# Neighbourhood-attention rows prepared for the output projection inside the retention stage, their value shares added by a small accumulating transfer per unit

## The chip, the cores and the metric

One core of one Trainium2 chip runs one whole layer of a hybrid diffusion backbone. The metric is the device time of that one launch in microseconds, taken as the median of several runs. The kernel before stands at 1739.89 us (three runs, 1737.87 to 1741.62).

## The reference, cut to what matters

The layer takes 1024 latent tokens of width 1024 and 256 context tokens. One input projection feeds two branches and two sets of gates; the branches are merged, projected and followed by a gated feed-forward network with a short convolution.

```
hx  = modulate(rmsnorm(x, norm1_g), sh1, sc1)             # 1024 x 1024
q, k, v, rq, rk, rv, rg, ga, gb = split(hx @ w_in)
o_na  = neighbourhood_attention(q, k, v, context k and v)  # 8 heads of 64: 1024 x 512, rows divided by the softmax sum
o_ret = norm(bi_retention(rope(rq), rope(rk), rv)) * silu(rg)   # 4 heads, chunks of 128
merged = sigmoid(ga) * (o_na @ w_proj_na) + sigmoid(gb) * (o_ret @ w_proj_ret)
x = x + g1 * (merged @ w_out)
x = x + g2 * conv_ffn(modulate(rmsnorm(x, norm2_g), sh2, sc2))
return rmsnorm(x, final_norm_g)
```

The change concerns `o_na`: how it gets from the attention to the product `o_na @ w_proj_na`.

## The kernel before, in words

Everything is kept transposed: channels on the 128 partitions, tokens along the free axis. A product in full fp32 precision is made of three TensorE (PE) matmuls: each operand is split into a rounded part ("hi", a copy to the type fp32r) and the rest ("lo", the difference), and hi·hi, hi·lo and lo·hi are summed. `split` (L90) does it, with the cast on ScalarE (ACT, L91) and the subtraction on VectorE (DVE, L92). `wload` (L102) fetches a 128x512 piece of a weight into a `raw` tile (three buffers, an SP transfer, L96) and splits it into a `wc` tile; `mm_a` (L121) runs such a product with the weights stationary (L115 to L117), `mm3` (L126 to L128) is a single product.

Stages in order of time: norms and adaLN (to 103 us), attention (103 to 370), retention (370 to about 690, with the gate columns of the input projection mixed into its last part), `pn` = `o_na @ w_proj_na` (702 to 754), the silu and merge gates (from 754), merge and output projection, feed-forward.

**Attention.** Four pairs of heads (`NPAIR`) by eight blocks of 128 tokens (`NJ`) give 32 units. A unit's values matmul yields, for two heads, a tile `rs` of 128 partitions: rows 0 to 63 and rows 64 to 127 are two shares of the same 64 channels (one from the hi, one from the lo half of V), which are to be added, and which lie in different partitions. `output` (L524 to L527) sends the two halves by two SP transfers of 64 KB to two planes of `d_ona` in DRAM. `rs` has two buffers. The softmax sums' reciprocals go to `d_r`.

**Retention.** Four heads of ten chunks: a `slot` (L1280) takes one front chunk of a head (projections, rotation, transposes, state products) together with one mixing chunk of the head before it; about 8 us each. In the front, ACT and DVE scale the keys into a tile `kz` (L1166 to L1171, two buffers) for the state product `dS` (L1173). The generator `shares` (L1264 to L1278) is advanced by one step per slot. Its first four steps each issue an accumulating POOL transfer of 512 KB that adds plane 1 of `d_ona` to plane 0 in DRAM. Its next sixteen steps handle eight pieces of 128x512: one step loads the sum (`osum`) and the reciprocals, spread over 64 partitions each (`rrep`), the next multiplies them on DVE (L1276) and writes the product back (L1277, a transfer on ACT's queue).

**Start of pn.** After the retention, eight loads `onr` (L1384) bring the scaled rows to SBUF in the column order of the gate stage (each row in pieces of 64 floats), and then all eight pieces are split in a row, ACT casting (L1388) and DVE subtracting (L1389), both with a permuting read (`perm`). The two `ona` tiles hold 128 x 4 x 1024 each. The loop (L1514 to L1533) then makes, for each of eight output blocks `db` and two halves of the tokens, twelve matmuls into a PSUM tile `pn`; the tile is multiplied by a gate `sgt` (loaded from `d_gate`, sigmoid on ACT) or copied, and stored in `d_pn`. Inside the loop `hx_sums` (L1365) makes the sums of blocks of hx for the Strassen-like gate products that follow: 4 POOL additions, 4 DVE additions and 4 splits, four times; its operands `hxT` are first read by PE right after pn's end.

**Order.** A list scheduler places the instructions of each engine ahead of time from modelled costs; those wrapped in `late` stay in the order in which they are written. Each engine then runs its own list strictly in order and waits for semaphores. DMA issues are instructions in such a list too: SP carries nearly all loads and stores, ACT some stores, POOL the accumulating ones. Pools are stacks of SBUF space: a pool opened later may take the space of a released one and then waits for its last users. `hcpool` holds the normalised context, which the retention still reads.

The rows that read kz and ona on PE:

```
for d in need:
    act.activation(kz[:, d, 0], k, AF.Copy, scale=self.dec(d))
    ...
    mm3(dS[:, d], kz[:, d, 0], kz[:, d, 1], v[:, 0], v[:, 1], True, True)
```

Of the kernel before, what the change touches and what calls it, by code (L numbers as in the profile page):

```python
# [8 lines left out]
F32 = mybir.dt.float32  # L9
F32R = mybir.dt.float32r  # L10
AF = mybir.ActivationFunctionType
ALU = mybir.AluOpType
# [4 lines left out]
P = 128  # L17
D = 1024
KB = D // P
T = 1024  # L20
# [5 lines left out]
NJ = 8  # L26
NA_HEADS = 8
HD = 64
NPAIR = NA_HEADS // 2
# [11 lines left out]
def tile_hybrid_layer(ctx, tc: tile.TileContext, io, dbg=None):  # L41
    nc = tc.nc
    vec, act, pool, pe, sync = nc.vector, nc.scalar, nc.gpsimd, nc.tensor, nc.sync

    def sb(name, side, bufs=1):
        return tc.alloc_tile_pool(name=name, bufs=bufs, side=side, reuse_waits="tile")
# [12 lines left out]
    d_gate = dram.tile([2 * KB, 2, P, 512], F32, name="d_gate")  # L59
# [61 lines left out]
    def mm_a(out, wcs, hi, lo):  # L121
        for _ in chain(out, wcs, hi, lo):
            pass
# [6 lines left out]
    def perm(ap, c):  # L130
        return ap.rearrange("p (j r c) -> p r j c", j=NJ, c=c)
# [215 lines left out]
    spilled = {}  # L347
# [24 lines left out]
    def local(ap, half):  # L372
        return ap[:, 0:T].rearrange("p (j x) -> p j x", j=NJ)[:, :, half * 64 : half * 64 + 64]
# [86 lines left out]
    class Unit:  # L460
# [61 lines left out]

        def output(self):
            pr, cs = self.pair.pr, slice(self.j * P, (self.j + 1) * P)  # L524
            for w in range(2):
                o = d_ona[pr, w].rearrange("(h d) q -> d h q", h=2)[:, :, cs]
                sync.dma_start(o, self.rs[w * HD : w * HD + HD])  # L527

    def ada_load():
        w = na.tile([P, D], F32, tag="aw", bufs=2, name="aw")  # L530
# [117 lines left out]
    with tc.manual_schedule():  # L648
# [300 lines left out]
        na = sb("na", "right")  # L949

        for shape, dt, tag, bufs in (
            ([P, 896], F32, "bias", 2),
            ([P, 16], F32, "st", 3),
            ([P, 640], F32, "P", 2),
            ([P, NJ + NCB, 2, 2, HD], F32R, "V", 1),
            ([P, 5, 2, P], F32R, "PT", 2),
            ([P, 2, P], F32, "rs", 2),
            ([P, 512], F32, "gs", 1),
        ):
            na.tile(shape, dt, tag=tag, bufs=bufs, name=tag)  # L960
# [77 lines left out]
        next(pieces, None)  # L1038

    us = []  # L1040
    for i in range(NPAIR * NJ + 1):
        live = i < NPAIR * NJ
        u1 = us[i - 1] if i >= 1 else None
        if i == 0:
            ada_load()
            ada_load()
        if i == 8:
            decays()
        for n in (0, 1) if i == 1 else (i,) if 1 < i < 32 else ():
            ada_col2(n)  # L1050
        if u1:
            if u1.j == 0:
                u1.pair.values()
            u1.transp(0)
        piece()
        if u1:
            u1.transp(1)
        if live:
            pair = pairs[i // NJ]
            if i % NJ == 0 and i:  # L1060
                pair.load_bias()
            us.append(Unit(pair, i % NJ))
            us[i].scores()
        if u1:
            u1.values()
            u1.output()
            puts(gate_sums, u1.st[:, 12:13], 1)
        piece()
        piece()
# [192 lines left out]


    def shares():  # L1264
        for pr in range(NPAIR):
            late(pool.dma_start(d_ona[pr, 0], d_ona[pr, 1], accum_op=ALU.add, max_dma_last_dim=8192))
            yield
        for pr in range(NPAIR):
            for half in range(2):
                cs = slice(half * 512, half * 512 + 512)  # L1270
                o, r = (rt.tile([P, 512], F32, tag="nrm", bufs=2, name=n) for n in ("osum", "rrep"))
                sync.dma_start(o, d_ona[pr, 0, :, cs])
# [4 lines left out]
                late(act.dma_start(d_ona[pr, 0, :, cs], o))  # L1277
                yield  # L1278

    def slot(main, mix, head=None, i=None):  # L1280
        def step():
# [73 lines left out]
    def g_ps(name):  # L1355
        return pg.tile([P, 512], F32, tag="g", bufs=6, name=name)

    def g_raw(name):
        return rr.tile([P, 512], F32, tag="r", bufs=10, name=name)

    hxT = {c: [tg.tile([P, KH, 512], F32R, name=f"hx{c}{i}") for i in range(2)] for c in ("T2", "T1", "T3", "T4")}
    ona = [onap.tile([P, NPAIR, T], F32R, name=f"ona{i}") for i in range(2)]


    def hx_sums(k):  # L1365
# [10 lines left out]
            split(hxT[c][0][:, k], hxT[c][1][:, k], src)  # L1376
        yield

    onr = []
    for half in range(2):  # L1380
        for pr in range(NPAIR):
            raw = g_raw("onr")
            src = d_ona[pr, 0].rearrange("p (j x) -> p j x", j=NJ)[:, :, half * 64 : half * 64 + 64]
            sync.dma_start(raw.rearrange("p (j x) -> p j x", j=NJ), src)  # L1384
            onr.append((pr, half, raw))
    for pr, half, raw in onr:
        dst = [ona[w][:, pr, half * 512 : half * 512 + 512].rearrange("p (r j c) -> p r j c", j=NJ, c=8) for w in range(2)]
        act.copy(dst[0], perm(raw, 8))  # L1388
        vec.tensor_tensor(dst[1], perm(raw, 8), dst[0].bitcast(F32), ALU.subtract)  # L1389


    def open3(out, ah, al, bh, bl, first, last):
# [118 lines left out]
    nsp = len(spilled) // 2  # L1511
    gu = [Gates("ret", h) for h in range(RH)] + [Gates("merge", db) for db in range(nsp, KB)]
    hs = None
    for db in range(KB):  # L1514
        if db % 2 == 0:
            hs = hx_sums(db // 2)
            next(hs)
        wp = [wpn[db] if db < 2 else wload(io["w_pna"][db, 0])]
        for half in range(2):
            sl_ = slice(half * 512, half * 512 + 512)  # L1520
            m = g_ps("pn")
            mm_a(m, wp, lambda k: ona[0][:, k, sl_], lambda k: ona[1][:, k, sl_])
            t = onap.tile([P, 512], F32, tag="pn", bufs=3, name="pnt")
            if (db, 0) in spilled:
                g = onap.tile([P, 512], F32, tag="sg", bufs=2, name="sgt")
                sync.dma_start(g, d_gate[2 * db, half])
                act.activation(g, g, AF.Sigmoid)
                vec.tensor_tensor(t, m, g, ALU.mult)
            else:
                act.copy(t, m)  # L1530
            sync.dma_start(d_pn[db, half], t)
# [49 lines left out]
    gr.release()  # L1581
    tg.release()
    rr.release()


    gpool = [sb(f"gates{i}", "right") for i in range(2)]
# [547 lines left out]
```

## Time and profile before

| | before |
|---|---|
| median of the runs | 1739.89 us |
| the profiled execution, its own time | 1738.33 us |
| its span, first to last instruction | 1736.6 us |
| mean granted TensorE clock | 0.997 |
| PE busy | 1713.1 us (99%) |
| DVE / ACT / POOL busy | 1223.9 / 824.6 / 548.2 us |
| transfers | 323.55 MB, 186 GB/s over the span |

PE is the engine that is nearly always busy; the others have room. The profile lists idle time in front of an instruction with what ended it, in square brackets in the timeline or as "idle before" in the groups. "PEclk" is the mean TensorE clock granted in a window, 1.00 being full speed, and "DMA share" the mean busy share of the sixteen DMA engines. "PEld" is the loading of weights, which overlaps the matmuls. A busy matmul at a lower clock counts as busy, so that a loss of that kind shows in the time that a number of matmuls takes, not in idle time. Lines are those of the kernel before.

### The profile page before, as it was taken

The numbers are of one execution on the slowest core, as the hardware profiler recorded it, in microseconds if no ns is written. First come the engines' busy times: TensorE is split into PE (matmuls) and PEld (weight loads), VectorE is DVE, ScalarE is ACT, GpSimd is POOL, SyncE is SP. The second block draws the span as 40 slices with busy tenths as digits, with TensorE's granted clock in tenths as the row PEclk, the third lists the DMA queues.
The fourth block names the chain that finished last, engine by engine and source line by source line (L and its number), as shares of the span: only waits on it lengthen the run. The fifth ranks groups of instructions, "written<-read, shape, count | busy, mean of one in ns | idle before, by whom it ended". The sixth has DMA issues, their size and how long they took to land.

```text
span 1736.6 us, 25162 instructions
## 1 busy us (share of the span) xinstructions
PE 1713.1 (99%) x8457; PEld 1425.9 (82%) x8457; DVE 1223.9 (70%) x2405; ACT 824.6 (47%) x1733; POOL 548.2 (32%) x710
## 2 busy tenths in 40 slices
PE   9999999999999999999999999999999999999998
PEld 7788888888888888688888888788888888888886
DVE  5777786655676766855555657877888888856756
ACT  6566665543343434453444324544444444544444
POOL 2100100013334343612222111013567656421444
PEclk9999999999999999999999999999999999999999
DMA  9255566546252323588876666768666776898744
GB/s 380 94 156 140 149 183 170 154 105 136 72 155 73 101 46 106 150 281 268 273 232 214 213 183 177 266 212 240 180 171 175 190 191 177 254 321 285 241 154 180
DMA packets 157761, 323.55 MB, mean 186 GB/s; under 512 B 28448, under 2 KB 45568, under 8 KB 151168
## 3 DMA queue, kind: packets, MB, share of 16 engines
q1 hardware_dynamic: 131824, 236.73, 41.1%
q0 software_dynamic: 12352, 72.37, 18.8%
q10 hardware_dynamic: 13456, 12.85, 2.2%
q8 instruction: 66, 1.08, 0.3%
q14 instruction: 63, 0.52, 0.1%
HBM read 257.07 MB, written 128.24 MB: 222 GB/s over the span
## 4 chain that ended last, share of the span: by engine, by line
PE 77%; DVE 6%; issue 6%; DMA 4%; POOL 3%; ACT 2%; SPq 0%; POOLq 0%; ACTq 0%; DVEq 0%
PE u L1394 28%; PE mm L117 4%; PE mm L115 4%; PE mm L116 4%; PE mm L128 3%; PE mm L126 3%; PE mm L127 3%; PE y L1394 2%; PE R L518 2%; PE ptp L500 2%; DMA ur<-d_a 2%; PE pr L116 2%; PE pr L115 2%; PE pr L117 2%; PE om L127 1%
## 5 line engine op out<-in xcount | busy, mean ns | idle before, releaser
L1394 PE MATMUL u<-T,wc 128*128 128x512 f32 x960 | 225.1, 390 | 0.6 <-ACT pu L1428 0.5
L1394 PEld LDWEIGHTS u<-T,wc 128*128 128x128 f32 x960 | 179.4, 188 | 40.6 <-ACT pu L1428 3.5
L1394 PE MATMUL y<-wc,ahl 128*128 128x512 f32 x924 | 210.1, 389 | 0.4 <-DVE wc L92 0.4
L1394 PEld LDWEIGHTS y<-wc,ahl 128*128 128x128 f32 x924 | 173.3, 188 | 36.8 <-DVE wc L92 0.8
L92 DVE TENSOR_TENSOR wc<-ur,wc 128x512 fp32r<-128x512 f32 x161 | 116.9, 729 | 61.7 <-ACT wc L91 61.7
L91 ACT CAST wc<-ur 128x512 fp32r<-128x512 f32 x161 | 99.6, 621 | 119.5 <-PE u L1394 71.9
L116 PE MATMUL mm<-low,wc 128*128 128x512 f32 (+1 forms) x312 | 119.2, 382 | 0.0
L1394 PE MATMUL u<-h2a,wc 128*128 128x512 f32 x480 | 112.8, 390 | 0.1
L115 PE MATMUL mm<-hx,wc 128*128 128x512 f32 x264 | 107.3, 407 | 0.2 <-ACT hc L229 0.2
L1394 PEld LDWEIGHTS u<-h2a,wc 128*128 128x128 f32 x480 | 89.8, 188 | 19.8 <-issue 0.7
L117 PE MATMUL mm<-hx,wc 128*128 128x512 f32 x264 | 104.9, 397 | 0.0
L1394 PE MATMUL u<-hxT,wc 128*128 128x512 f32 x384 | 89.6, 389 | 0.0
L583 POOL COPY pad<-pu 128x1 f32<-128x1 f32 x54 | 36.6, 678 | 156.5 <-DVE pu L1431 116.4
L583 POOL COPY pad<-st 128x1 f32<-128x1 f32 x32 | 5.9, 185 | 251.9 <-DVE st L491 244.4
L1394 PEld LDWEIGHTS u<-hxT,wc 128*128 128x128 f32 x384 | 72.1, 188 | 15.0
L91 ACT CAST wc<-raw 128x512 fp32r<-128x512 f32 x86 | 53.2, 622 | 55.0 <-DMA raw<-in_w_ret 10.4
L92 DVE TENSOR_TENSOR wc<-raw,wc 128x512 fp32r<-128x512 f32 x86 | 60.7, 711 | 18.5 <-ACT wc L91 17.8
L128 PE MATMUL mm<-wc,low 128*128 128x512 f32 (+1 forms) x180 | 68.9, 383 | 0.0
L91 ACT CAST wc<-s 128x512 fp32r<-128x512 f32 x56 | 34.8, 622 | 70.6 <-PE u L1394 70.6
L116 PEld LDWEIGHTS mm<-low,wc 128*128 128x128 f32 x312 | 59.1, 189 | 7.2
L1170 ACT ACTIVATE kz<-r,dec 128x128 fp32r<-128x128 f32 x72 | 27.9, 400 | 76.4 <-POOL r L1151 76.1
L1394 PE MATMUL u<-hx,wc 128*128 128x512 f32 x192 | 61.9, 390 | 0.0
(411 smaller groups left out, 4731.9 us busy)
## 6 DMA issues: line engine op xcount, KB each, us to landing
d_a<-at SPq DMA_DIRECT2D x77, 256.0 KB, 3.2
ur<-d_a SPq DMA_DIRECT2D x77, 256.0 KB, 5.3
ur<-in_w_up SPq DMA_DIRECT2D x74, 256.0 KB, 7.1
d_w<-in_w_down POOLq DMA_DIRECT2D x66, 256.0 KB, 7.3
aw<-in_w_ada SPq DMA_DIRECT2D x32, 512.0 KB, 3.8
d_a<-d_a POOLq DMA_DIRECT2D x44, 256.0 KB, 7.3
ur<-d_w SPq DMA_DIRECT2D x44, 256.0 KB, 3.8
d_s<-in_w_up POOLq DMA_DIRECT2D x36, 256.0 KB, 5.9
```

Source lines behind the costliest of these rows:

```text
L91: act.copy(hi, src)
L92: (lo_eng or vec).tensor_tensor(lo, src, hi.bitcast(F32), ALU.subtract)
L115: pe.matmul(out, wh, xh, start=k == 0, stop=False)
L116: pe.matmul(out, wh, xl, start=False, stop=False)
L117: pe.matmul(out, wl, xh, start=False, stop=k == n - 1)
L126: pe.matmul(out, ah, bh, start=first, stop=False)
L127: pe.matmul(out, ah, bl, start=False, stop=False)
L128: pe.matmul(out, al, bh, start=False, stop=last)
L500: pe.transpose(tp[:, c], self.Pm[h][:, c * P : (c + 1) * P], ident)
L518: pe.matmul(R[:, h], self.pair.V[:, g, h].rearrange("p a b -> p (a b)"), self.PT[h][:, c].rearrange("p a b -> p (a b)"), start=c == 0, sto ...
L583: late(pool.tensor_copy(tick, src))
L1394: pe.matmul(out, a, b, start=first and n == 0, stop=last and n == 2, skip_group_check=True)
```

## The change

Four things are done.

1. A unit's second share is no longer stored in a plane of its own. It is added by an accumulating POOL transfer of the same size to what SP has just stored, in the one plane that `d_ona` now has. The four large accumulating transfers of the retention go. The `rs` tiles get another place in SBUF.
2. `shares` has eight rounds of two steps: the loads (now in the column order of the gate stage, in pieces of 64 floats), then multiplication, cast (into the buffer of `rrep`) and subtraction (into a new tile `olo`, which shares the two buffers of the tag `kz`). The two parts go to a new DRAM tensor `d_on` by two transfers on ACT's queue, in the step after. All of it stays in the order written.
3. The splitting at the start of pn is gone. The two parts come straight from `d_on`: for the first half of the tokens into a pool `ona0`, which is opened where `hcpool` is released and has its size, and for the second half into the pool `onap` as before.
4. The loop over pn goes by groups of four `db` and by halves: four blocks with the first half, the same four with the second, then the other four blocks in the same way. Four weight pieces are loaded ahead of it (two before), and the steps of `hx_sums` fall on n = 0, 4, 8, 12 and n = 1, 5, 9, 13.

```diff
-    d_ona = dram.tile([NPAIR, 2, P, T], F32, name="d_ona")
+    d_ona = dram.tile([NPAIR, P, T], F32, name="d_ona")
+    d_on = dram.tile([2, 2, NPAIR, P, 512], F32, name="d_on")
...
-            for w in range(2):
-                o = d_ona[pr, w].rearrange("(h d) q -> d h q", h=2)[:, :, cs]
-                sync.dma_start(o, self.rs[w * HD : w * HD + HD])
+            o = d_ona[pr].rearrange("(h d) q -> d h q", h=2)[:, :, cs]
+            sync.dma_start(o, self.rs[0:HD])
+            late(pool.dma_start(o, self.rs[HD:P], accum_op=ALU.add))
...
     def shares():
-        for pr in range(NPAIR):
-            late(pool.dma_start(d_ona[pr, 0], d_ona[pr, 1], accum_op=ALU.add, max_dma_last_dim=8192))
-            yield
-        for pr in range(NPAIR):
-            for half in range(2):
-                cs = slice(half * 512, half * 512 + 512)
+        for half in range(2):
+            for pr in range(NPAIR):
                 o, r = (rt.tile([P, 512], F32, tag="nrm", bufs=2, name=n) for n in ("osum", "rrep"))
-                sync.dma_start(o, d_ona[pr, 0, :, cs])
+                part = lambda t: t.rearrange("p (j x) -> p j x", j=NJ)
+                late(sync.dma_start(part(o), local(d_ona[pr], half)))
                 for h in range(2):
-                    sync.dma_start(r[h * HD : h * HD + HD], d_r[pr, h : h + 1, cs].to_broadcast([HD, 512]))
+                    late(sync.dma_start(part(r[h * HD : h * HD + HD]), local(d_r[pr, h : h + 1].to_broadcast([HD, T]), half)))
                 yield
                 late(vec.tensor_tensor(o, o, r, ALU.mult))
-                late(act.dma_start(d_ona[pr, 0, :, cs], o))
+                hi, lo = (t.rearrange("p (r j c) -> p r j c", j=NJ, c=8) for t in (r.bitcast(F32R), rt.tile([P, 512], F32R, tag="kz", bufs=2, name="olo")))
+                late(act.copy(hi, perm(o, 8)))
+                late(vec.tensor_tensor(lo, perm(o, 8), hi.bitcast(F32), ALU.subtract))
                 yield
+                for w, t in enumerate((hi, lo)):
+                    late(act.dma_start(d_on[w, half, pr].rearrange("p (r j c) -> p r j c", j=NJ, c=8), t.bitcast(F32)))
...
-    wpn = [wload(io["w_pna"][db, 0]) for db in range(2)]
+    wpn = [wload(io["w_pna"][db, 0]) for db in range(4)]
...
+    onp = sb("ona0", "right")
...
-    ona = [onap.tile([P, NPAIR, T], F32R, name=f"ona{i}") for i in range(2)]
+    ona = [[p_.tile([P, NPAIR, 512], F32R, name=f"ona{half}{i}") for i in range(2)] for half, p_ in enumerate((onp, onap))]
...
-            raw = g_raw("onr")
-            src = d_ona[pr, 0].rearrange("p (j x) -> p j x", j=NJ)[:, :, half * 64 : half * 64 + 64]
-            sync.dma_start(raw.rearrange("p (j x) -> p j x", j=NJ), src)
-            onr.append((pr, half, raw))
-    for pr, half, raw in onr:
-        dst = [ona[w][:, pr, half * 512 : half * 512 + 512].rearrange("p (r j c) -> p r j c", j=NJ, c=8) for w in range(2)]
-        act.copy(dst[0], perm(raw, 8))
-        vec.tensor_tensor(dst[1], perm(raw, 8), dst[0].bitcast(F32), ALU.subtract)
+            for w in range(2):
+                sync.dma_start(ona[half][w][:, pr].bitcast(F32), d_on[w, half, pr])
...
-    for db in range(KB):
-        if db % 2 == 0:
-            hs = hx_sums(db // 2)
+    for n, (db, half) in enumerate([(db, half) for d0 in range(0, KB, 4) for half in range(2) for db in range(d0, d0 + 4)]):
+        if n % 4 == 0:
+            hs = hx_sums(n // 4)
             next(hs)
-        wp = [wpn[db] if db < 2 else wload(io["w_pna"][db, 0])]
...
+        if n >= 4 and n < 8:
+            wpn.append(wload(io["w_pna"][n, 0]))
+        m = g_ps("pn")
+        mm_a(m, [wpn[db]], lambda k: ona[half][0][:, k], lambda k: ona[half][1][:, k])
...
-        if db % 2 == 0:
+        if n % 4 == 1:
             next(hs)
```

The order of the instructions on an engine moves at three places that matter below. In these rows a number in front is the line in the kernel they are of; the changed kernel's lines stand one or two higher than those of the kernel before (L91 is L92 there, L1170 is L1171).

First, ACT at the passage from the first head to the second, before (`wx` and `wc` are weight pieces being cast, `kz` the scaled keys, `ds`, `SS`, `r` and `v` parts of the states, the rotation and the values):

```order
L1136 CAST v<-mm 128x256
L91 CAST wx<-raw 128x512 x2
L1170 ACTIVATE kz<-r_4957,dec 128x128
L1192 COPY ds<-dS 128x256
L1201 CAST SS<-st 128x256
L91 CAST wc<-raw 128x512
L1161 CAST qk<-tp 128x256
L1136 CAST v<-mm 128x256
L1192 COPY ds<-dS 128x256
L91 CAST wc<-raw 128x512
L1141 COPY r_5061<-mm 128x128
L1170 ACTIVATE kz<-r_5061,dec 128x128 x2
```

and now:

```order
L1193 COPY ds<-dS 128x256
L1202 CAST SS<-st 128x256
L1162 CAST qk<-tp 128x256
L1276 CAST rrep<-osum 128x512
L1137 CAST v<-mm 128x256
L1171 ACTIVATE kz<-r_4971,dec 128x128
L92 CAST wx<-raw 128x512
L92 CAST wc<-raw 128x512
L1142 COPY r_5078<-mm 128x128
L92 CAST wc<-raw 128x512
L1193 COPY ds<-dS 128x256
L1171 ACTIVATE kz<-r_5078,dec 128x128 x2
```

The first `kz` of these stood behind two weight casts and stands now behind one of them (just ahead of these rows) and behind the cast of a share's rows (`rrep<-osum`); the second pair stands behind three weight casts, as before. On PE, the first `dS` product of this place stands seven matmuls further back than before, behind the first products of the next head.

Second, ACT at the start of pn, before (`gs` is a gate column's result, `sgt` a gate, `hxT` the operands of the gate stage):

```order
L361 COPY gs<-mm 128x512
L91 CAST wc<-raw 128x512
L362 DMA d_gate<-gs 128x512
L1388 CAST ona_8404<-onr 128x512 x8
L1527 ACT_TABLE_LOAD
L1527 ACTIVATE sgt<-sgt 128x512 x2
L91 CAST hxT_8398<-b 128x512
```

and now:

```order
L362 COPY gs<-mm 128x512
L92 CAST wc<-raw 128x512
L363 DMA d_gate<-gs 128x512
L92 CAST hxT_8440<-b 128x512
L92 CAST hxT_8442<-b 128x512
L92 CAST hxT_8438<-b 128x512
L92 CAST hxT_8444<-b 128x512
L1522 ACT_TABLE_LOAD
L1522 ACTIVATE sgt<-sgt 128x512 x2
L92 CAST wc<-raw 128x512 x2
```

The eight casts are gone, and the casts for the gate stage stand ahead of the first two gates.

Third, SP ahead of pn, now (`ona_8448` and `ona_8449` are the hi and lo part of the second half of the tokens; the eight transfers of the first half stand ahead of these rows, before the last `in_w_gate` load):

```order
L97 DMA raw<-in_w_gate 128x512
L97 DMA raw<-in_w_pna 128x512 x8
L1385 DMA ona_8448<-d_on 128x512
L1385 DMA ona_8449<-d_on 128x512
L1385 DMA ona_8448<-d_on 128x512
L1385 DMA ona_8449<-d_on 128x512
L1385 DMA ona_8448<-d_on 128x512
L1385 DMA ona_8449<-d_on 128x512
L1385 DMA ona_8448<-d_on 128x512
L1385 DMA ona_8449<-d_on 128x512
L1521 DMA sgt<-d_gate 128x512 x2
```

Before, SP had the eight `onr` loads behind six of the `in_w_pna` loads and the other two behind them; now all eight `in_w_pna` loads come first and the second half of the rows follows.

More of the change, by code (lines that the diff above doesn't have):

```diff
@@ L1040, in tile_hybrid_layer @@
     us = []
+    na.tile([P, 2, P], F32, tag="rs", bufs=2, name="rs")
     for i in range(NPAIR * NJ + 1):
@@ L1513, in tile_hybrid_layer @@
     hs = None
-    for db in range(KB):
-        if db % 2 == 0:
-            hs = hx_sums(db // 2)
+    for n, (db, half) in enumerate([(db, half) for d0 in range(0, KB, 4) for half in range(2) for db in range(d0, d0 + 4)]):
+        if n % 4 == 0:
+            hs = hx_sums(n // 4)
             next(hs)
-        wp = [wpn[db] if db < 2 else wload(io["w_pna"][db, 0])]
[L1519 to L1531, printed above, removed]
-        if db % 2 == 0:
+        if n >= 4 and n < 8:
+            wpn.append(wload(io["w_pna"][n, 0]))
+        m = g_ps("pn")
+        mm_a(m, [wpn[db]], lambda k: ona[half][0][:, k], lambda k: ona[half][1][:, k])
+        t = onap.tile([P, 512], F32, tag="pn", bufs=3, name="pnt")
+        if (db, 0) in spilled:
+            g = onap.tile([P, 512], F32, tag="sg", bufs=2, name="sgt")
+            sync.dma_start(g, d_gate[2 * db, half])
+            act.activation(g, g, AF.Sigmoid)
+            vec.tensor_tensor(t, m, g, ALU.mult)
+        else:
+            act.copy(t, m)
+        sync.dma_start(d_pn[db, half], t)
+        if n % 4 == 1:
             next(hs)
@@ L1583, in tile_hybrid_layer @@
     rr.release()
+    onp.release()
     gpool = [sb(f"gates{i}", "right") for i in range(2)]
```

2 lines of the change are left out of this document (removed).

## The prediction, as it was put on record before the changed kernel ran

> **What bounds the kernel now.** The page comes first, then PE's waits, then windows and the timeline where a wait stood out. PE is busy for 99% of the span:
>
> ```profile
> span 1736.6 us, 25162 instructions
> PE 1713.1 (99%) x8457; PEld 1425.9 (82%) x8457; DVE 1223.9 (70%) x2405; ACT 824.6 (47%) x1733; POOL 548.2 (32%) x710
> ```
>
> So a change that takes no matmul away (this one does not) can win only PE's idle 23.5 us (1736.6 less 1713.1) and whatever PE loses while it counts as busy. PE's waits, grouped by line (total us, times, longest):
>
> ```profile
> PE dS L126 <- ACT kz L1170: 5.5, 4, 2.0
> PE pn L116 <- DVE ona L1389: 1.8, 4, 0.7
> PE pn L115 <- ACT ona L1388: 1.7, 1, 1.7
> ```
>
> The change edits the places of all three. By idle time the start of pn is worth 3.5 us. But its idle time is not its loss. The windows of pn's own instructions (the last three numbers: granted clock, DMA share, GB/s) show the first 24 matmuls and the other 168 (169 were recorded there, one of them at the border):
>
> ```profile
> 702.35:716.34 13.99, 10.20 (x24) 5.43 (x25) 0.00 (x0) 0.00 (x0) 0.76 0.38 118
> 716.34:754.46 38.12, 38.12 (x169) 31.35 (x167) 5.45 (x8) 2.83 (x5) 1.00 0.61 196
> ```
>
> At the undisturbed pace, 38.12/168 = 0.227 us each, 24 matmuls take 5.45 us. They took 13.99. **The start of pn loses 8.5 us**, of which only 3.5 are idle. The rest is a lower clock, seen in the windows of all work:
>
> ```profile
> 705.00:710.00 5.00, 4.61 (x11) 2.73 (x12) 5.00 (x4) 3.11 (x7) 4.95 (x3) 0.62 0.45 138
> 710.00:715.00 5.00, 4.48 (x11) 2.03 (x9) 5.00 (x4) 2.13 (x3) 5.00 (x4) 0.70 0.00 0
> ```
>
> The timelines of PE, ACT and DVE say why PE starves there: the eight casts stand in ACT's list behind the last gate column's copy, and DVE then needs 1.43 us for each subtraction.
>
> ```profile
> 704.22 0.50 PE L115 MATMUL pn<-ona,wc 128*128 128x512 f32 x1 [1.71 <-ACT ona L1388]
> 702.54 0.59 ACT L361 COPY gs<-mm 128x512 f32<-128x512 f32 x1 [1.00 <-PE mm L117]
> 703.55 4.26 ACT L1388 CAST ona<-onr 128x512 fp32r<-128x512 f32 x8
> 704.29 11.43 DVE L1389 TENSOR_TENSOR ona<-onr,ona 128x512 fp32r<-128x512 f32 x8
> ```
>
> The other place is the passage from one retention head to the next (PE, then ACT):
>
> ```profile
> 431.30 0.39 PE L126 MATMUL dS<-v,kz 128*128 128x256 f32 x1 [1.90 <-ACT kz L1170]
> 438.89 0.39 PE L126 MATMUL dS<-v,kz 128*128 128x256 f32 x1 [1.31 <-ACT kz L1170]
> 515.52 0.39 PE L126 MATMUL dS<-v,kz 128*128 128x256 f32 x1 [1.96 <-ACT kz L1170]
> 430.85 0.40 ACT L1170 ACTIVATE kz<-r,dec 128x128 fp32r<-128x128 f32 x1
> 437.62 0.62 ACT L91 CAST wc<-raw 128x512 fp32r<-128x512 f32 x1 [4.47 <-DMA raw<-in_w_ret]
> ```
>
> The kz that PE wants is not late by itself. It is queued behind weight casts, and those wait for weights whose transfers are slow while large accumulating transfers are in flight, the third of them issued at 422.10, the last at 428.2:
>
> ```profile
> 422.10 1.06 POOL L1266 DMA_DIRECT2D d_ona<-d_ona  x1
> 425.00:430.00 5.00, 4.40 (x26) 4.04 (x24) 2.48 (x10) 0.62 (x1) 3.02 (x6) 1.00 1.00 284
> 422.83 7.47 DMA raw<-in_w_ret
> raw<-in_w_ret SPq DMA_DIRECT2D x32, 256.0 KB, 3.5
> ```
>
> The chain of waits has one of these weight loads at 7.47 us, where the median of 32 is 3.5.
>
> **The change part by part.**
>
> *Start of pn.* Both sets of eight splits leave it; what remains must be in SBUF in time. The first half needs only the released context space, and its eight loads stand on SP between gate weights of the retention's end, tens of microseconds early. The second half is needed four blocks later, at 702.35 + 48 × 0.227 = 713.2 us. Its loads stand behind all `in_w_pna` loads, the last of which needs the raw tile that a subtraction frees at about 701.2 (the cast at 699.44 and the subtraction at 700.50 + 0.68 below). A contiguous load costs SP about 0.33 us to issue (the row of `osum`), so the eighth is issued at about 704; 2 MB at the 301 GB/s of that stretch are 7.0 us: landed by about 709, four microseconds ahead. If each issue cost the 1.09 us of the old `onr` loads and landed after their longest 7.8, the last would come at 701.2 + 8.7 + 7.8 = 717.7; that is the first rival. I take 709, since the new transfers have the form of the cheap row, not pieces of 64 floats.
>
> ```profile
> 699.44 0.62 ACT L91 CAST wc<-raw 128x512 fp32r<-128x512 f32 x1 [2.11 <-PE mm L117]
> 700.50 0.68 DVE L92 TENSOR_TENSOR wc<-raw,wc 128x512 fp32r<-128x512 f32 x1
> L1272 SPq DMA_DIRECT2D osum<-d_ona x8: 326/326/332, 414.2 to 568.3; - x8
> L1384 SPq DMA_DIRECT2D onr<-d_ona x8: 619/1090/1498, 688.2 to 696.9; - x8
> DMA to landing us min/median/max: 4.3/5.0/7.8
> 700.00:705.00 5.00, 3.01 (x13) 1.72 (x11) 2.49 (x5) 2.90 (x7) 0.41 (x1) 1.00 1.08 301
> ```
>
> Then pn has no wait at its start: **−8.5 us**.
>
> *What stands behind pn* comes 8.5 us earlier. The sums of hx end on DVE at 746.99 + 1.89 = 748.9, and PE reads the first at 757.29; moved up, it would read at 748.8. So even if DVE finished no sooner it would cost 0.1 us, and DVE is freed of 11.43. Cost: nothing.
>
> ```profile
> 746.99 1.89 DVE L92 TENSOR_TENSOR hxT<-b,hxT 128x512 fp32r<-128x512 f32 x3
> 757.29 2.88 PE L1394 MATMUL u<-hxT,wc 128*128 128x512 f32 x12
> ```
>
> *Attention.* SP issues 32 transfers fewer, POOL 32 more. At the old accumulating transfer's 0.83 to 1.06 us that is at most 34 us on an engine that is busy for 25.81 of these 267. POOL's own copies and weight transfers queue behind each, which waits about 2.1 us for the first share to land; none of them feeds the attention. An `rs` tile is held until the accumulation has landed: 2.1 + 1.06 + 8.7 = 11.9 us at the worst of the old large ones. Units are (368.4 − 103.8)/31 = 8.5 us apart and there are two tiles, so a tile is wanted after 17. PE waits for nothing in this stage (266.68 of 267 busy). Cost: nothing.
>
> ```profile
> 103.00:370.00 267.00, 266.68 (x1614) 230.61 (x1613) 196.98 (x537) 163.70 (x471) 25.81 (x65) 1.00 0.56 155
> L527 SPq DMA_DIRECT2D d_ona<-rs x64: 574/598/1276, 103.8 to 368.4; - x64
> DMA to landing us min/median/max: 2.0/2.1/3.8
> L1266 POOL DMA_DIRECT2D d_ona<-d_ona x4: 831/1046/1065, 408.3 to 428.2; - x4
> DMA to landing us min/median/max: 5.9/7.7/8.7
> ```
>
> *Retention.* Eight casts and eight subtractions come here, at the 0.62 and 0.68 to 1.78 us that they have now, against ACT and DVE loads of 64.03 and 108.83 in 150 us: room in sum. What matters is the order. A share's cast stands in ACT's list ahead of a kz, so a late share holds up PE through it. In a round of two slots the two parts are sent out (3.5 us to landing), the next `rrep` is loaded into the freed tile (5.0 for pieces of 64 floats, as the `onr` rows have it), then multiplied: 3.5 + 5.0 = 8.5 against one slot of about 8. That chain just fits, and `olo` takes one of the two kz tiles meanwhile.
>
> ```profile
> 440.00:590.00 150.00, 147.74 (x791) 127.27 (x790) 108.83 (x357) 64.03 (x188) 62.99 (x98) 1.00 0.40 108
> L1277 ACTq DMA_DIRECT2D d_ona<-osum x8: 332/365/368, 459.9 to 582.9; - x8
> DMA to landing us min/median/max: 2.0/3.5/5.0
> ```
>
> At the first passage, with the parts sent at about 422, the share is multiplied at about 431, cast, and then kz comes at about 432.3, later than the 430.85 that the 431.30 row answers to; PE has seven products of 384 columns ahead of it there, 7 × 0.227 × 384/512 = 1.2 us. So the wait of 1.90 stays at about 2.2. The wait of 1.31 behind it goes, as the weights no longer share the engines with the accumulation. The passage at 515 I leave as it is (−0 of 1.96). Net **−1.0**. Bounds: all dS waits gone, −5.4 (of 5.5); or a wait of 1.90 in each of the eight rounds, 15.2 in place of 3.2, +12.0. I take a value near the lower end because ACT has 4 us of idle time ahead of each kz in the steady slots, an example being this row:
>
> ```profile
> 475.90 0.41 ACT L1170 ACTIVATE kz<-r,dec 128x128 fp32r<-128x128 f32 x1 [4.28 <-POOL r L1151]
> ```
>
> **The sum**, against the profiled execution's own 1738.33 us (span 1736.6 and 1.7 around it): −8.5 − 1.0 = −9.5, so 1728.8. That execution lies 1.6 under the median of 1739.89; set against the median, **1730.4 us**.
>
> **The rivals.** *The second half comes late.* If SP pays the old 1.09 us per issue, rows for the last product of the block (due at 713.2 + 9 × 0.227 = 715.2) land at 717.7: 2.5 us idle. Then the clock may fall again as it did after a gap of 1.71: the 20 matmuls of the two windows of low clock took (4.61 + 4.48)/20 = 0.45 us each in place of 0.227, and 15 such cost 3.4 more. −9.5 + 5.9 = −3.6: 1736.3. For it speaks the DMA share of 1.08 around 700; against it, the contiguous form.
>
> The Trainium skill ("TensorE: Matmul & The Clock Gate", Part 1) has the clock halved only after an idle window of about 3.4 us. Here 0.62 followed an idle time of 1.71 us, which does not agree. By the page this rival would lose 2.5 alone, and come out at about 1733.
>
> *The gain is given back at the gates.* PE arrives 8.5 us earlier and the gate weights, prepared by transfers, do not: DMA runs at 0.61 in pn and at 0.87 after. Paid back in full this is −1.0: 1738.9. Against it: PE does not wait at all in the 46 us after pn, and the transfers have 0.39 to spare before.
>
> ```profile
> 754.00:800.00 46.00, 46.00 (x205) 38.00 (x204) 23.54 (x35) 19.46 (x33) 11.64 (x22) 1.00 0.87 282
> ```
>
> *Slower: the shares hold up the retention.* With the chain of 8.5 us in a slot of 8 and kz down to one tile, every round makes PE wait 1.90, +12.0 − 8.5 = +3.5: 1743.4. It decides the sign from (8.5 + 3.2)/8 = 1.5 us a round on. Against it stand ACT's 4 us.
>
> *All dS waits go*, since the large transfers do: −8.5 − 5.4, 1726.0.
>
> **How the numbers follow.** My forecast 0.64, the late second half 0.14, the gates 0.06, the retention 0.08, all dS waits gone 0.08. Two tenths of a per cent, 3.5 us, is about what can be told from no change, so faster means under 1736.4: the forecast, the best case and most of the late half, 0.84; within it 0.09 (the gates and some of the late half); slower 0.07. The range leaves out the gates and the retention and reaches from just under the best case to just over the late half: 1725 to 1737.
>
> **What would show it.** Right: pn's first 24 matmuls take about 5.5 us at clock 1.00, no pn matmul waits for `ona`, and the wait of `dS` for kz falls from 5.5 to about 4.5. The late half would show as a pn wait for a transfer at about 713 to 715 and a clock under 1.00 after it; the retention as waits of dS for kz in most of the eight rounds, behind `rrep` casts; the gates as PE waits from about 746 on. The forecast is wrong if pn starts without a wait and the time still falls by less than 6 us: then something that I cost at nothing was not free.

## The result

The changed kernel takes 1730.15 us (median of four runs, 1727.25 to 1731.11), the kernel before 1739.0 beside it. The medians lie 8.9 us apart, which is 0.51%. The ratio on record, over all these runs, is 0.9944 with a 95% interval of 0.9927 to 0.9962, or 0.56% faster. The forecast was 1730.4. The total is as predicted; several of its terms are not, and they missed in opposite directions. That they cancelled is luck, and it is what the rest of this document is about.

The page of the changed kernel:

```profile
span 1727.8 us, 25181 instructions
PE 1707.8 (99%) x8457; PEld 1426.2 (83%) x8457; DVE 1223.1 (71%) x2405; ACT 825.3 (48%) x1733; POOL 577.7 (33%) x738
```

and the waits of PE in it that bear on the change (total us, times, longest):

```profile
PE pn L116 <- DVE pnt L1523: 4.0, 3, 2.0
PE dS L127 <- ACT kz L1171: 2.2, 1, 2.2
...
PE dS L129 <- DVE kz L1172: 0.5, 1, 0.5
```

No pn matmul waits for `ona` any more, and the dS waits have fallen from 5.5 us to 2.7. In their place stands a wait that the kernel before did not have: pn waits for `pnt`, the product with the gate that empties a PSUM tile. The windows of pn's instructions, cut again after the first 24 matmuls:

```profile
698.90:704.35 5.45, 5.42 (x24) 4.50 (x24) 0.00 (x0) 0.00 (x0) 1.00 0.79 230
704.35:747.82 43.47, 39.32 (x169) 31.04 (x167) 5.21 (x8) 4.10 (x7) 1.00 0.61 202
```

The first 24 take 5.45 us at full clock, to the hundredth what the prediction worked out, in place of 13.99. But the other 168, 38.12 us before, take 43.47, of which 43.47 − 39.32 = 4.15 are idle. The profile's own account of the 8.8 us between the two profiled executions is this (pn's start is where PE is first free for it, its waiting included in pn):

| | before | changed | difference | predicted |
|---|---|---|---|---|
| pn begins | 702.35 | 698.90 | −3.45 | −1.0 |
| first 24 matmuls of pn | 13.99 | 5.45 | −8.5 | −8.5 |
| the other 168 | 38.12 | 43.47 | +5.35 | 0 |
| behind pn, to the end of the span | 982.1 | 980.0 | −2.1 | 0 |
| span | 1736.6 | 1727.8 | −8.8 | −9.5 |

### The profile page after: what moved, and what is told of

It reads as the page before. It is cut to its first block, busy times and chain, and to the rows that moved or that the text cites. A ratio compares the mean times of both kernels' runs of the same rounds, so it can differ in the third digit from the quotient of the medians.

```text
span 1727.8 us, 25181 instructions
## 1 busy us (share of the span) xinstructions
PE 1707.8 (99%) x8457; PEld 1426.2 (83%) x8457; DVE 1223.1 (71%) x2405; ACT 825.3 (48%) x1733; POOL 577.7 (33%) x738
## 4 chain that ended last, share of the span: by engine, by line
PE 45%; issue 5%; DMA 3%; POOL 2%; DVE 2%; ACT 1%; SPq 0%; POOLq 0%; ACTq 0%; DVEq 0%
PE u L1390 29%; PE y L1390 2%; DMA ur<-d_a 2%; PE om L129 2%; PE om L127 2%; PE om L128 2%; PE pr L118 2%; PE pr L116 2%; PE pr L117 2%; PE u L117 1%; PE u L118 1%; PE u L116 1%; POOL x L1939 1%; DMA d_a<-at 1%; POOL pd L1976 0%
## 5 line engine op out<-in xcount | busy, mean ns | idle before, releaser
L92 ACT CAST wc<-ur 128x512 fp32r<-128x512 f32 x161 | 99.6, 620 | 119.9 <-PE u L1390 70.0
L528 POOL DMA_DIRECT2D d_ona<-rs x32 | 31.6, 988 | 241.7 <-DVE st L492 73.7
L92 ACT CAST wc<-raw 128x512 fp32r<-128x512 f32 x86 | 53.2, 622 | 42.8 <-PE pr L118 9.6
L93 DVE TENSOR_TENSOR wc<-raw,wc 128x512 fp32r<-128x512 f32 x86 | 65.6, 769 | 11.0 <-ACT wc L92 10.4
L92 ACT CAST wc<-s 128x512 fp32r<-128x512 f32 x56 | 34.9, 622 | 69.3 <-PE u L1390 67.1
L92 ACT CAST wc<-wr 128x512 fp32r<-128x512 f32 x56 | 34.7, 621 | 60.2 <-PE u L1390 43.2
```

What stands on the lines that cost most here:

```text
L92: act.copy(hi, src)
L93: (lo_eng or vec).tensor_tensor(lo, src, hi.bitcast(F32), ALU.subtract)
L528: late(pool.dma_start(o, self.rs[HD:P], accum_op=ALU.add))
```

## The experiments

### Four gate tiles, and another order of the blocks

The loop multiplies the first eight groups by gates that are loaded into two tiles `sgt`. In the changed kernel the first of the three waits is at the ninth group. There are six PSUM tiles, so its tile is that of the third group. PE's three rows, then ACT's, DVE's and SP's at the time, and two later ones of DVE (the number of instructions in a row is behind the x):

```profile
722.01 0.50 PE L116 MATMUL pn<-ona,wc 128*128 128x512 f32 x1 [0.72 <-DVE pnt L1523]
729.82 0.50 PE L116 MATMUL pn<-ona,wc 128*128 128x512 f32 x1 [2.04 <-DVE pnt L1523]
736.80 0.50 PE L116 MATMUL pn<-ona,wc 128*128 128x512 f32 x1 [1.25 <-DVE pnt L1523]
714.15 1.16 ACT L1522 ACTIVATE sgt<-sgt 128x512 f32<-128x512 f32 x2
720.60 1.26 ACT L1522 ACTIVATE sgt<-sgt 128x512 f32<-128x512 f32 x2 [4.27 <-DMA sgt<-d_gate]
714.81 1.29 DVE L1523 TENSOR_TENSOR pnt<-pn,sgt 128x512 f32<-128x512 f32 x2 [0.33 <-ACT sgt L1522]
721.26 1.32 DVE L1523 TENSOR_TENSOR pnt<-pn,sgt 128x512 f32<-128x512 f32 x2 [3.23 <-ACT sgt L1522]
716.54 0.91 SPq L1521 DMA_DIRECT2D sgt<-d_gate  x2
727.40 1.76 DVE L93 TENSOR_TENSOR hxT<-b,hxT 128x512 fp32r<-128x512 f32 x1
729.09 1.28 DVE L1523 TENSOR_TENSOR pnt<-pn,sgt 128x512 f32<-128x512 f32 x2
```

The products free the tiles at 716.1, SP issues the next two loads at 716.54, ACT has them at 720.60, DVE multiplies at 721.26: this round of two groups takes 6.45 us, where PE makes two groups in 24 × 0.227 = 5.45. The next two rounds take 7.83 and 6.96 us (products at 729.09 and 736.05). The longest wait, 2.04, ends with the product at 729.09, and that one did not wait for its gate: the sigmoid was done at 726.4, but the product stands in DVE's list behind work on the sums of hx, of which the last subtraction is shown, and DVE had no pause before it. So the rounds are made of the gates' loads, in the first and the third, and of the hx sums, in the second. Two edits, each of the changed kernel, take this away in different ways. The first gives the gates four tiles, paid for by two raw tiles of the same stage:

```diff
-        return rr.tile([P, 512], F32, tag="r", bufs=10, name=name)
+        return rr.tile([P, 512], F32, tag="r", bufs=8, name=name)
...
-            g = onap.tile([P, 512], F32, tag="sg", bufs=2, name="sgt")
+            g = onap.tile([P, 512], F32, tag="sg", bufs=4, name="sgt")
```

> The changed kernel with four tiles for the loaded gates in place of two (two raw tiles of the gate stage fewer). Theory: the three waits of pn behind pnt (4.0 us, with the refills after them about 5.3) come from the gates' two tiles: a tile is loaded again only when its product is done, and a round of load, sigmoid and product takes longer than two groups on PE. Then these waits fall under 1 us, pn takes about 44 to 45 us in place of 48.9, and the time falls by 4 to 5 us against the changed kernel, to about 1725. Rival: the first sigmoid, late behind the casts of the hx sums, sets the chain; then the waits stay at 2 us or more. Second rival: what pn wins is lost at the gates behind it, and the time stays at 1730.

Measured: 1724.68 us, ratio 0.9921 (0.9903 to 0.9940). The window of pn's instructions shows no wait left:

```profile
697.90:741.43 43.53, 43.53 (x192) 35.83 (x191) 5.12 (x8) 4.08 (x7) 1.00 0.73 249
```

192 × 0.227 = 43.6, so this is pn at its full pace. The second edit leaves two tiles and takes the output blocks in another order, so that every second group needs a gate:

```diff
-    wpn = [wload(io["w_pna"][db, 0]) for db in range(4)]
+    wpn = {db: wload(io["w_pna"][db, 0]) for db in (0, 4, 1, 5)}
...
-    for n, (db, half) in enumerate([(db, half) for d0 in range(0, KB, 4) for half in range(2) for db in range(d0, d0 + 4)]):
+    for n, (db, half) in enumerate([(db, half) for dbs in ((0, 4, 1, 5), (2, 6, 3, 7)) for half in range(2) for db in dbs]):
...
-            wpn.append(wload(io["w_pna"][n, 0]))
+            wpn[(2, 6, 3, 7)[n - 4]] = wload(io["w_pna"][(2, 6, 3, 7)[n - 4], 0])
```

> The changed kernel with two tiles for the gates as it has, but the order of the output blocks 0, 4, 1, 5 and 2, 6, 3, 7 in place of 0 to 3 and 4 to 7, so that every second group needs a gate in place of the first eight in a row. Theory (two tiles feed one gated group per about 3.2 us): with a gated group only every 5.4 us the waits go; pn takes 44 to 45 us and the time falls by 4 to 5 us, to about 1725. Rival (the late first sigmoid): a copied group stands behind it on the same engine, and a wait of 1 to 2 us stays.

Measured: 1725.8 us, ratio 0.9925 (0.9910 to 0.9939); pn takes 44.06 us with one wait of 0.17. Both intervals overlap a little with the changed kernel's (0.9927 to 0.9962); pn's 43.5 and 44.1 us against its 48.9 leave no doubt of the place. Two independent ways of easing the gates' round remove the wait. The late first sigmoid alone is not what held pn: with the other order of blocks it comes as late as in the changed kernel, 15.3 us behind pn's beginning in both. (With four tiles it comes after 13.0.) So the 5.35 us are the price of eight gated groups in a row with two gate tiles and the hx sums in between, once PE no longer comes late. What the place of the hx sums in DVE's list costs by itself, no run shows.

### The splits put back

The changed kernel with the one difference that the shares are only scaled in the retention and written as one part, and that the casts and subtractions stand before pn again:

```diff
-                late(act.copy(hi, perm(o, 8)))
-                late(vec.tensor_tensor(lo, perm(o, 8), hi.bitcast(F32), ALU.subtract))
                 yield
-                for w, t in enumerate((hi, lo)):
-                    late(act.dma_start(d_on[w, half, pr].rearrange("p (r j c) -> p r j c", j=NJ, c=8), t.bitcast(F32)))
+                late(act.dma_start(d_on[0, half, pr], o))
...
+            raw = g_raw("onr")
+            sync.dma_start(raw, d_on[0, half, pr])
...
+        act.copy(dst[0], perm(raw, 8))
+        vec.tensor_tensor(dst[1], perm(raw, 8), dst[0].bitcast(F32), ALU.subtract)
```

> The changed kernel with the splits put back at the start of pn: the shares are only scaled in the retention and written as one part, and eight loads, eight casts and eight subtractions stand before pn, as in the kernel before; the new order of pn and the accumulation per unit stay. Theory: the start of pn loses its 8.5 us again, but the later PE arrival takes up the gate waits of 4 to 5.3 us, so the time rises by only 3 to 4.5 us against the changed kernel, to about 1734. Rival: the two losses add up, +8.5, to about 1738.5.

Measured: 1730.93 us, ratio 0.9952 (0.9937 to 0.9967), not to be told from the changed kernel. pn begins at 697.64, 1.3 us earlier than with the splits in the retention, and its window shows 50.69 us:

```profile
697.64:748.33 50.69, 47.12 (x192) 37.76 (x192) 5.34 (x8) 3.49 (x6) 0.93 0.62 205
```

The expectation was 3 to 4.5 us more; it came nearer to none. pn as a whole loses 50.69 − 43.6 = 7.1 us here, the gates take 5.35 in the changed kernel, and the changed kernel reaches pn 1.3 us later: what the move of the splits is worth with two gate tiles is 7.1 − 5.35 − 1.3 = 0.5 us between these two profiles. The 1.3 us are not a clean price of the splits in the retention, for the changed kernel's profile has some 1.6 us of low clock there (see "The shares later").

The same with four gate tiles was meant to complete a square of four kernels:

> The kernel with the splits put back at the start of pn and four gate tiles as well. With it four kernels differ in two things only: where the splits are (start of pn, retention) and how many gate tiles there are (two, four). Theory: moving the splits was worth little with two tiles (1730.9 against 1730.15) because the gates then bound pn, and is worth its price with four: this kernel has no gate waits to lose, so it stays at 1730 to 1731, against 1724.7 with the splits moved, and pn takes 50 to 51 us. Rival: the gate tiles alone bring the gain; then it comes to about 1726.

Measured: 1735.05 us, ratio 0.9969 (0.9957 to 0.9982). It is slower than expected. pn takes 52.75 us, with a new wait of 1.42 us for a weight's subtraction in the middle, where DVE is late. I take it that the two raw tiles that were given up are needed in this kernel, since the eight `onr` take all eight, but no run shows it. So the square is not clean: 0.9969 against 0.9921 would be 8.3 us for the move of the splits, but some of it may be the price of the raw tiles. A better comparison leaves this kernel out. With the splits put back and two gate tiles pn never waited for `pnt`, so that more gate tiles had no such wait to take away. Against that kernel, the one with four gate tiles and the splits moved ends pn 6.9 us earlier (741.43 against 748.33) and has a median 6.25 us lower, with intervals that hardly overlap (0.9903 to 0.9940, 0.9937 to 0.9967). With four gate tiles the move is worth several times the 0.5 us.

### The first part alone

The kernel before, with only the accumulating transfer per unit; the four steps of the large transfers stay, empty:

```diff
-            for w in range(2):
-                o = d_ona[pr, w].rearrange("(h d) q -> d h q", h=2)[:, :, cs]
-                sync.dma_start(o, self.rs[w * HD : w * HD + HD])
+            o = d_ona[pr].rearrange("(h d) q -> d h q", h=2)[:, :, cs]
+            sync.dma_start(o, self.rs[0:HD])
+            late(pool.dma_start(o, self.rs[HD:P], accum_op=ALU.add))
...
         for pr in range(NPAIR):
-            late(pool.dma_start(d_ona[pr, 0], d_ona[pr, 1], accum_op=ALU.add, max_dma_last_dim=8192))
             yield
```

> The kernel before with the first part of the change alone: the second share is added by an accumulating transfer per unit, the four large accumulating transfers of the retention are gone (their four steps stay, empty), all the rest is as before, the splits at the start of pn too. Theory: the weights that came late behind the large transfers come in time, so the waits of dS at the first passage between heads (1.90 and 1.31 us) fall under 1 us together, while the wait at the second passage (1.96) stays, since SP's order there (two weight loads behind a share's load) is as before; pn starts 2 to 3 us earlier and the time falls by 2 to 3 us, to about 1737. Rival: the waits do not come from the large transfers; the time stays at 1739.4.

Measured: 1734.67 us, ratio 0.9969 (0.9955 to 0.9983). Both waits of the first passage between heads are gone. The order of ACT's list there is the same, but the eight weight loads of the passage landed after 2.5 to 4.9 us, with a median of 3.5, where in the kernel before they took 2.5 to 8.6 with a median of 5.8. So the waits came from the large transfers. The wait at the second passage stays and is longer, as the timelines of PE, ACT and SP show:

```profile
511.84 0.58 PE L126 MATMUL dS<-v,kz 128*128 128x256 f32 x1 [2.37 <-ACT kz L1170]
510.87 0.62 ACT L91 CAST wc<-raw 128x512 fp32r<-128x512 f32 x1 [4.91 <-DMA raw<-in_w_ret]
503.06 1.46 SPq L96 DMA_DIRECT2D raw<-in_w_ret  x2
```

The pieces of weight that ACT waits for were issued behind a share's load on SP, and they also took long: 7.6 and 7.8 us to land, where the median of the eight loads there is 3.8. pn begins only 1.3 us earlier than before, and not 2 to 3 as was expected; the time falls by 6.1 us in the medians and by 3.3 in the spans, where 2 to 3 were expected. One profiled execution can stand that far from the median.

A second finding of this run is worth more than the first. The start of pn is that of the kernel before, and loses as much, at full clock. The window of its first matmuls:

```profile
701.10:715.17 14.07, 7.78 (x25) 4.34 (x26) 0.00 (x0) 0.00 (x0) 1.00 0.37 124
```

and two rows of PE's timeline in it:

```profile
709.31 0.50 PE L116 MATMUL pn<-ona,wc 128*128 128x512 f32 x1 [0.73 <-DVE ona L1388]
711.00 0.50 PE L116 MATMUL pn<-ona,wc 128*128 128x512 f32 x1 [0.73 <-DVE ona L1388]
```

14.07 us for the same first matmuls at a clock of 1.00, against 13.99 at 0.76. The eight subtractions take 11.44 us here and 11.43 before. The later ones end 1.69 us apart, and three matmuls wait for each. So DVE's pace sets the length of this stretch, and in the kernel before the low clock only filled time in which PE would have waited.

### The order on SP at the second passage

The same with three empty steps in place of four, which puts six weight loads in a row on SP at the second passage:

```diff
-        for pr in range(NPAIR):
+        for pr in range(NPAIR - 1):
             yield
```

> The kernel before with the first part of the change alone and the shares one slot earlier (three empty steps ahead of them in place of four). SP then has six weight loads in a row at the second passage between heads, where it had two of them behind a share's load of the sums and two more behind that share's reciprocals. Theory: the wait of dS at the second passage (1.96 us in the kernel before, 2.37 with the first part alone) comes from that order on SP; it falls under 0.5 us, and no dS wait over 0.5 us is left. The start of pn still loses 8 to 8.5 us, whether its clock falls or not. The time falls by 2 to 4 us against the first part alone. Rival: the weights are late there whatever the order, because the transfers are busy; then a wait of 1.5 us or more stays.

Measured: 1731.84 us, ratio 0.9960 (0.9946 to 0.9974). The wait falls from 2.37 to 0.92 us, with 0.44 for the subtraction behind it. That is between the theory (under 0.5) and the rival (1.5 and more). So moving the shares by a slot takes away a part of this wait. Whether it does so through the order on SP or through what else is in flight is not told apart: the slowest weight load there took 6.5 us in place of 7.8. The start of pn still loses its time, 14.10 us for the first 24 matmuls at full clock. The interval overlaps that of the first part alone, so the gain in time is not shown.

In the changed kernel the passage stands better still (0.50, and no weight load over 3.9 us), and there SP issues three of the weight pieces in a row from 501.73, ahead of the share's load at 508.41 (SP's timeline):

```profile
501.73 4.23 SPq L97 DMA_DIRECT2D raw<-in_w_ret  x3
508.41 0.56 SPq L1270 DMA_DIRECT2D osum<-d_ona  x1
```

### The shares later

The changed kernel, with no share at the first passage:

```diff
-            if (h == 0 and i >= NCB + 4) or (h in (1, 2) and i >= NCB):
+            if (h == 0 and i >= NCB + 7) or (h in (1, 2) and i >= NCB):
```

> The changed kernel with its shares started three slots later, so that no share's cast stands in the passage from the first head to the second. Theory: the one wait left there (2.25 us of dS for kz) is due to the share (its rows come late, and its cast stands ahead of kz): it falls under 0.5 us and the time falls by about 2 us, to 1728. Rival: it is due to the weight pieces that land late in front of their cast there; then it stays at 1 to 2 us.

The wait that this is about, in the changed kernel, with ACT's two rows ahead of it:

```profile
432.79 0.58 PE L127 MATMUL dS<-v,kz 128*128 128x256 f32 x1 [2.25 <-ACT kz L1171]
431.55 0.62 ACT L1276 CAST rrep<-osum 128x512 fp32r<-128x512 f32 x1 [0.51 <-DVE osum L1274]
432.34 0.40 ACT L1171 ACTIVATE kz<-r,dec 128x128 fp32r<-128x128 f32 x1
```

Measured: 1727.91 us, ratio 0.9936 (0.9921 to 0.9951). No dS wait is left over 0.2 us, and pn begins at 695.1 in place of 698.9. That is 3.8 us, more than the wait of 2.25. The rest is the clock, which in the changed kernel fell behind that wait, as this window of 1 us of all work shows:

```profile
433.00:434.00 1.00, 1.00 (x4) 0.50 0.21 80
```

Of the 3.8 us at pn, 2.2 remain in the medians and 0.3 in the spans. The interval overlaps most of the changed kernel's (0.9927 to 0.9962), so that the gain is seen in the profile only. The stages behind pn, which no edit touches, take from 980.0 us (the changed kernel) to 984.2 (this one) over the profiled executions here; I take this for scatter and not for an effect of the shares, though no run shows it.

### Both gains together

Four gate tiles and the later shares:

> The changed kernel with four gate tiles and the shares started three slots later. Theory: both gains add up. No wait of dS behind kz over 0.5 us, pn about 43.3 us from a start at about 695, in all about 2 us less than with four gate tiles alone (1724.7): 1722 to 1723. Rival: what is won ahead is lost in the stages behind pn, and it stays at 1724.7.

Measured: 1723.7 us, ratio 0.9904 (0.9889 to 0.9919), the fastest of all, though 1722 to 1723 were expected; its profiled execution took 1720.55. pn begins at 694.2 and has no wait, and no dS wait is left over 0.2. Against four gate tiles alone the intervals overlap (0.9903 to 0.9940), so that the second gain is seen in the profile and not yet in the times. Against the changed kernel they do not: the two edits take about 0.4% more off it.

## Why the prediction came out right, point by point

**The start of pn, −8.5: right in size, wrong in its reason.** The waits for `ona` are gone and the first 24 matmuls take 5.45 us. But "the rest is a lower clock" does not hold: the first part alone loses the same at full clock. The step would have been right as "DVE needs 11.43 us for the eight subtractions, and PE cannot pass it".

**What stands behind pn, nothing: wrong.** This is the step that failed. It looked at one thing that pn's loop makes, the sums of hx, and not at the other, the gated products that empty PE's own PSUM tiles. In the kernel before, the loss at the start gave these products the time they needed; without the loss they became the bound and took 5.35 us back. The trace of before had the numbers. Its seventh product (DVE's timeline) was this one:

```profile
740.38 0.68 DVE L1528 TENSOR_TENSOR pnt<-pn,sgt 128x512 f32<-128x512 f32 x1
```

It ended at 741.06, and the thirteenth group, which reuses its PSUM tile, began at 716.34 + 120 × 0.227 = 743.6. That is 2.5 us of room for a PE that was to come 8.5 us earlier. If the products had come no sooner, PE would have stood still for about 6 us, by this estimate; they came somewhat sooner.

**The second half in time: right.** Its loads were issued from 700.70 to 704.3, and no matmul waited for them. The groups of both halves' loads, by their line:

```profile
L1385 SPq DMA_DIRECT2D ona<-d_on x16: 330/430/738, 587.6 to 704.3; - x16
DMA to landing us min/median/max: 2.6/5.2/6.4
```

At 0.43 us an issue and 6.4 us at most to landing they were there by 710.7; the first of them was needed at 698.9 + 10.9 = 709.8, the last later. The rival of a late second half fell. Its price was also a little too high: the two windows of low clock list 11 matmuls each, one of them at the border, so that 21 and not 20 share the 9.09 us, and the rival comes to about 1736.0 in place of 1736.3.

**Attention, nothing: right.** The POOL transfers, by their line:

```profile
L528 POOL DMA_DIRECT2D d_ona<-rs x32: 966/977/1243, 106.6 to 372.0; - x32
DMA to landing us min/median/max: 2.7/3.2/5.3
```

They land well inside the bound of 8.7 us, and PE's first wait behind the attention is at 373.03, before at 373.16.

**Retention, −1.0: right at the first passage, wrong at the second, and not closed.** kz was forecast at 432.3 and came at 432.34; the wait was forecast at about 2.2 and is 2.25; the wait behind it is gone, as was said. The step that failed is leaving "the passage at 515 as it is": three weight loads come ahead of the share's load on SP there, the slowest weight load took 3.9 us in place of 7.4, and the wait of 1.96 became 0.50. The forecast also did not count the clock behind the first wait, which costs the changed kernel about 1.6 us. Measured −3.45. These parts do not add up to it: up to pn PE's idle time fell from 9.51 to 6.68 us, and the busy time of the same 3964 matmuls fell by 0.6 although the low clock is in it, so that some 2.2 us of busy time stay without an account. The rival by which the shares hold up PE in every round fell: only one of the eight costs more than 0.5 us.

**Behind pn, 0: −2.1.** 1.0 us of it is there by the first of the 480 `h2a` products of the feed-forward's main loop (L1394, 1134.2 before, 1126.6 now, so −7.6 against −6.6 at pn's end), and two waits for `h2l` on the way to it (1.1 us) became one (0.3). Over the executions profiled here this stretch takes 980.0 to 984.2 us, so I take it as scatter.

**The sum.** −3.45 − 8.5 + 5.35 − 2.1 = −8.7 (−8.8 in the spans, by rounding), against −9.5. The gates gave back 5.35 us that the forecast did not know of, and the retention and scatter brought 4.6 that it did not know of either. That the two nearly cancel is luck. The rival "given back at the gates" had the right idea at the wrong place: the gates inside pn, not those behind it. A prediction of the total could not show that; the profile's waits did.

What carried the change follows from the runs. The kernel with the splits put back is as fast, so with two gate tiles their move is worth about 0.5 us between the profiles and nothing that the times show. What the change brought came from its other parts: the small accumulating transfers, which alone give a ratio of 0.9969, and the orders of the shares, of SP and of pn that came with them, which no run took apart to the end. In the kernels run here, the move of the splits paid where the gates had room.

## What to carry to other kernels

Where a stall on the bounding engine is taken away, list every loop that shares the stage and ask for its own period: buffers, load, two engines, against the time PE needs for as many groups. A loop with two buffers that is hidden behind a stall can become the bound when the stall goes, and here two more buffers, or spreading its groups, were worth more than moving the splits was without them. A total that agrees is no proof of its terms; compare stage by stage.

## What the runs showed of the hardware that was not expected

Between 100 and 1710 us, the granted clock of the ten profiled kernels falls to one half in pieces of one length or twice that. Added up from windows of 1 us, it is about 3.4 us in the changed kernel (432.7 to 436.1), in the one with the other order of blocks and in the one with the shares one slot earlier, and 6.8 in the kernel before, in the first part alone and in both kernels with the splits put back. In the three others there is none. What sets it off is not the length of one idle stretch. It fell behind waits of 1.71 (before), 2.25 (the changed kernel) and 2.37 us (the first part alone), and in the kernel with the shares one slot earlier behind 0.92 and 0.44 shortly after one another, but not behind 2.45 us in the kernel with four gate tiles, nor behind the 2.04 of pn in the changed kernel. The Trainium skill ("TensorE: Matmul & The Clock Gate", Part 1) has free-running windows of about 3.4 us, which agrees with the lengths here; that a whole idle window is needed does not agree. Half the clock over 3.4 us is worth some 1.7 us. That this can change from one execution of the same program to the next is likely but not shown, for each kernel has one profile; the mean granted clocks of sixteen executions of the kernel before do differ, from 0.994 (1744.13 us) to 0.999 (1736.54 us).
